# Moving the sums of repeated experts' gates from the routing to the table writes, holding gathers back until the routing is over, and pacing the zeroing

## The chip, the cores and the metric

One NeuronCore of a Trainium2 chip runs the whole program. The metric is device microseconds of one launch; before the change the median of three runs is 4929.35 us (4927.22 to 4931.84). TensorE (PE) does the matrix products, VectorE (DVE) and ScalarE (ACT) the elementwise work, GpSimd (POOL) some elementwise work and all indirect DMAs, and SyncE (SP) issues the plain DMAs.

## The reference: what is computed

Two layers of a diffusion backbone over 512 latent tokens and 256 context tokens (six tiles of 128 tokens), width 1024. Each layer has a modulated norm, one wide input projection, three kinds of attention heads, an output projection with a gated residual, and then PEER, a retrieval of single-neuron experts: 16,384 experts, 8 heads, the best 16 experts of each head for each token.

```
q = (x @ Wq) per head, in two halves; scores of 128 + 128 keys; top 16 of each; top 16 of the sums
e[t, h, k]   expert number,   g[t, h, k] = softmax of the chosen scores
y[t] = sum over h, k of  g[t,h,k] * gelu(x[t] . U[e[t,h,k]]) * V[e[t,h,k]]
```

The kernel computes the sum over experts as dense products wherever that is cheaper: a "P" array or a "table" holds, per token, a number for each of the 16,384 experts, zero nearly everywhere. If two heads of a token choose the same expert, its entry has to hold the sum of both gates. Those sums are what this change moves.

## The kernel before, in words

Layer 0 handles tiles 0 to 5, layer 1 (the last) tiles 0 to 3, since context tokens are not read again. After the attention part of a layer come four stages:

- **Up pass, half 0 and half 1** (`upass`): 64 steps `jj` each. A step loads 512 KB of U, splits it in a high and a low fp16 half (`hl`, on ACT and DVE, or POOL in the first steps) and multiplies with the tokens of the tiles that are done densely (`pw` in half 0, `pa` in half 1, 24 matmuls a step).
- **Value pass, group by group** (`vpass`): 128 steps a group; a step loads 512 KB of V, splits it into `hl` too, and multiplies with the weights of three tiles (layer 0: tiles 2, 3, 4, then 5, 0, 1) or two (layer 1) into `acc`.

The routing (scores, top 16, gates: `routing`, `pick`) runs beside half 0 as a list of generators, `rg`; a step of `upass` advances it by `RRATE`. Three ways lead from the routing to the value pass:

- Tiles 2 and 3 use one-hot products on PE (`Onehot`).
- Tiles 4 and 5 of layer 0 and tile 1 of layer 1 ("dense, with a table") write the gates into a table in DRAM, 8 MB a tile. `Table.clear` zeroes it with 8 DMAs of 1 MB. `Table.put` writes one head: 16 indirect DMAs on POOL, called *puts* below, L1266, `table<-gs,to`, whose offsets are `to` and whose values are `gs`.
- Tiles 0 and 1 of layer 0 and tile 0 of layer 1 ("picked") skip the dense up pass. For each of their 128 experts a token, `gather` reads 128 rows of U by one indirect DMA of 512 KB on POOL (L946, `r<-peer_u,ix`), and DVE makes a dot product with the token (L952, 1024 columns). There are 3 buffers `r`. After 16 dots, gelu and the gate follow, and 16 puts of `a` into the tile's table. All dots of a tile go into one `a`, so the second tile's dots wait for the first tile's last puts.

In all there are 384 gathers and 768 puts. Gathers stand in the list `bg` and puts in the list `sq` (first come first served); a step of `upass` or `vpass` advances them by `RATES[layer]` and `SRATES[layer]`, whose four numbers in use are those of half 0, half 1 and the two groups of the value pass. Every gather and put is tied behind the latest split `hl` by an ordering edge without a semaphore (`queue_behind`), so that the compiler's scheduler, which sorts each engine's instructions by priority, does not pull it to the front. Each engine then runs its queue in that order.

The gate sums are made in `pick` (L921, tile `gjk`): for each of the 128 chosen experts of a token one DVE instruction compares it with all 128 (`is_equal`), multiplies with the gates and adds up. It does so for each of the six tiles that have a table (four in layer 0, two in layer 1), right after the routing of that tile, 768 in all.

Of the kernel before, what the change touches and what calls it, by code (L numbers as in the profile page):

```python
# [31 lines left out]
RATE_NA, RATE_DF = 2.7, 1.4  # L32
RATES = {0: (0.8, 1.0, 1.5, 1.5, 0.0, 0.0), 1: (0.6, 1.2, 0.4, 0.8, 0.0, 0.0)}
SRATES = {0: (2.0, 2.9, 1.6, 1.8, 4.0, 4.0), 1: (1.5, 1.8, 0.9, 1.2, 4.0, 4.0)}
RRATE = (1.3, 1.05)
# [6 lines left out]
ZC = 2048  # L42
# [5 lines left out]
class Hybrid:  # L48
# [22 lines left out]
    def consts(self):  # L71
# [13 lines left out]
        self.tok = c.tile([128, 1], F32, name="tok")  # L85
        nc.gpsimd.iota(self.tok, pattern=[[0, 1]], base=0, channel_multiplier=1, allow_small_or_imprecise_dtypes=True)
        self.mhalf = c.tile([128, 8], F32, name="mhalf")
        nc.vector.memset(self.mhalf, -0.5)
# [181 lines left out]
    def mixers(self, l, last, wes):  # L270
# [11 lines left out]
        with ExitStack() as e:  # L282
            nap = self.pool(e, "nqkv")
            self.naT = nap.tile([128, 4, 2, T], F16, name="naT")
            self.nav = [nap.tile([128, 2, 2, 256], F16, name=f"nav{p}") for p in range(3)]
            self.zero = nap.tile([128, ZC // 4], F32, name="zero")
            self.nc.gpsimd.memset(self.zero, 0.0)
            hp = self.pool(e, "hT", 3)
# [75 lines left out]
    def project(self, l, last, hp, pool, ps, ap_, att_es, xs):  # L364
# [3 lines left out]
        def load(ch):  # L368
            res = []
            for k in range(0, KC, 2):  # L370
                w = pool.tile([128, 2, 256], F32, name="wst", bufs=3)
                nc.sync.dma_start(w, wv[:, k:k + 2, ch * 256:ch * 256 + 256])
                h = pool.tile([128, 2, 256], F16, name="wh", bufs=6)
                lo = pool.tile([128, 2, 256], F16, name="wl", bufs=6)
                self.wsplit(h, lo, w)
                res += [(h[:, x], lo[:, x]) for x in range(2)]
            return res
# [441 lines left out]
    def picks(self, l, tiles, sv, si, pool):  # L819
        for t in tiles:  # L820
            yield from self.pick(l, t, sv[t], si[t], pool)
            if t in self.picked:
                self.bg.append(self.gather(l, t))
            elif t in self.tables:
                self.sq += [self.tables[t].put(h, self.rt[t][2], self.rt[t][0], h, 8) for h in range(8)]

# [21 lines left out]
    def pick(self, l, t, sv, si, pool):  # L848
# [25 lines left out]
        st = pool.tile([128, 2, 16, 8], F16, name="st")  # L874
        sg = pool.tile([128, 16, 8], F32, name="sgate")
        sh = [128, 16, 16, 8]
# [27 lines left out]
        if t not in self.tables:  # L904
            self.onehot.prep(t, st.rearrange("p a k h -> p a (k h)"), sg.rearrange("p k h -> p (k h)"))
            self.rt[t] = None
            return
        ef = pool.tile([128, 16, 8], F32, name="ef")
        nc.vector.scalar_tensor_tensor(ef, st[:, 0], 128.0, st[:, 1], op0=OP.mult, op1=OP.add)
        ix = None  # L910
        if t in self.picked:
            ix = self.lp.tile([128, 16, 8], I32, name="ix", bufs=len(self.picked))
            nc.vector.tensor_scalar(ix, ef, float(l * 16384), None, op0=OP.add)
        to = self.lp.tile([128, 16, 8], I32, name="to", bufs=len(self.tables))
        nc.vector.tensor_scalar(to, ef, 128.0, self.tok, op0=OP.mult, op1=OP.add)

        gs = self.lp.tile([128, 16, 8], F32, name="gs", bufs=len(self.tables))
        e, g, o = (z.rearrange("p k h -> p (k h)") for z in (ef, sg, gs))
        for k in range(128):
            jk = pool.tile([128, 128], BF16, name="gjk")  # L920
            nc.vector.scalar_tensor_tensor(jk, e, e[:, k:k + 1], g, op0=OP.is_equal, op1=OP.mult,  # L921
                                           accum_out=o[:, k:k + 1])
            if k % 16 == 15:
                yield
        self.rt[t] = o, ix, to

# [9 lines left out]
    def gather(self, l, t):  # L936
        nc = self.nc
        gs, ix, to = self.rt[t]
        h = self.lp.tile([128, D], F32, name="hg", bufs=1)
# [3 lines left out]
        for k in range(128 + AHEAD):  # L943
# [6 lines left out]
            if k >= AHEAD:  # L950
                r, d = rows[k - AHEAD], k - AHEAD
                nc.vector.scalar_tensor_tensor(r, r, 1.0, h, op0=OP.mult, op1=OP.mult,  # L952
                                               accum_out=a[:, d // 16, d % 16:d % 16 + 1])
                if d % 16 == 15:
                    x = a[:, d // 16]
                    nc.scalar.activation(x, x, AF.Gelu)
                    nc.vector.tensor_tensor(x, x, gs[:, d // 16::8], op=OP.mult)
                    self.sq.append(self.tables[t].put(d // 16, to, x, 0, 1))
            yield
# [64 lines left out]
    def upass(self, l, half, ps, tag, rrate, more=None):  # L1024
# [18 lines left out]
        for jj in range(64):  # L1043
# [24 lines left out]
            self.tick(self.rg, rrate)  # L1068
            self.tick(self.bg, RATES[l][half])
            self.tick(self.sq, SRATES[l][half])  # L1070
# [163 lines left out]
class Table:  # L1234
# [19 lines left out]
    def clear(self):  # L1254
        o = self.o
        for c in range(0, 128 * 128, ZC):
            self.before.append(o.nc.sync.dma_start(self.view()[:, c:c + ZC].rearrange("i (r n) -> i r n", r=4),
                                                  o.zero[:, None].to_broadcast([128, 4, ZC // 4])))
            yield

    def put(self, h, to, values, c, step):
        o = self.o
        key = f"{self.key}_{h}"
        now = []
        for k in range(16):
            ins = o.nc.gpsimd.indirect_dma_start(  # L1266
                out=self.d, out_offset=bass.IndirectOffsetOnAxis(ap=to[:, k, h:h + 1], axis=0),
                in_=values[:, c + step * k:c + step * k + 1], in_offset=None)
            if k:
# [85 lines left out]
```

## Time and profile before

| | |
|---|---|
| median of 3 runs | 4929.35 us (4927.22 to 4931.84) |
| profiled run | 4932.08 us, span of the trace 4930.0 us, mean granted TensorE clock 0.921 |
| layer 0: attention part | 0 to 611 us |
| layer 0: up pass, half 0 / half 1 | 611 to 1186 / 1186 to 1618 us |
| layer 0: value pass, group 1 / group 2 | 1618 to 2437 / 2437 to 2944 us |
| layer 1: attention part | 2944 to 3405 us |
| layer 1: up pass, half 0 / half 1 | 3405 to 3875 / 3875 to 4191 us |
| layer 1: value pass | 4191 to 4930 us |

The stages' times come from the starts of their first splits `hl`. Times are microseconds from the start of the span. "Busy" is time in which an engine works; "idle before" is time in which it stood still just before an instruction, with what ended that time behind the arrow ("issue": nothing that the profile shows). A granted clock of 1.00 is TensorE at 2.4 GHz; a smaller number is a stretch in which part of the time was granted at 1.2 GHz.

### The profile page before, as it was taken

What the parts mean: (1) busy time and instruction counts of PE and PEld (TensorE: products, weight loads), DVE (VectorE), ACT (ScalarE), POOL (GpSimd) and SP (SyncE); (2) the same over time, 40 slices, a digit from 0 to 9 for tenths busy, and PEclk for the clock granted to TensorE, in tenths of its full rate; (3) what the DMA queues carried; (4) which work ended last, traced back from release to release, by engine and by line L of the source; (5) the groups of instructions that cost most, each with busy time, mean ns of one, the idle gap of its engine ahead of it and who ended that gap; (6) DMA issues with size and microseconds to landing.
All of it is one profiled execution on the core that took longest, in us unless ns stands there. A gap on an engine that the chain in (4) does not pass through costs nothing. (4 is left out here: it accounts for less than half of the span.)

```text
span 4930.0 us, 74817 instructions
## 1 busy us (share of the span) xinstructions
PE 4154.8 (84%) x27326; PEld 2287.3 (46%) x27326; DVE 3391.1 (69%) x7913; ACT 1981.4 (40%) x3236; POOL 1877.5 (38%) x1536
## 2 busy tenths in 40 slices
PE   4987888987898889567599999978879888999998
PEld 3664453753444334222244447745546445444443
DVE  7677559889555776566466554574698867987665
ACT  4556353432222334112233336564525322554444
POOL 4224214303777774567500002251213577761000
PEclk8997898998999989878799999978989999999999
DMA  7831343324667887977778863114446678777887
GB/s 250 298 127 35 131 124 100 111 75 129 196 207 214 256 263 224 337 262 262 228 252 269 259 219 102 50 42 135 125 127 190 214 255 267 264 259 253 265 270 238
DMA packets 512322, 971.54 MB, mean 197 GB/s; under 512 B 73824, under 2 KB 295488, under 8 KB 511952
## 3 DMA queue, kind: packets, MB, share of 16 engines
q1 hardware_dynamic: 422464, 759.66, 48.0%
q0 software_dynamic: 80032, 201.86, 12.8%
q10 hardware_dynamic: 9456, 5.24, 0.4%
q8 instruction: 214, 3.51, 0.3%
q14 instruction: 156, 1.28, 0.1%
HBM read 861.77 MB, written 104.78 MB: 196 GB/s over the span
## 5 line engine op out<-in xcount | busy, mean ns | idle before, releaser
L1141 PE MATMUL acc<-hl,gst 128*128 128x512 f16 x7680 | 1761.7, 391 | 231.2 <-ACT gst L140 151.7
L1141 PEld LDWEIGHTS <-gst 128*128 128x128 f16 x7680 | 760.8, 100 | 1201.4 <-issue 179.6
L1054 PEld LDWEIGHTS <-hl 128*128 128x128 f16 x6144 | 613.3, 101 | 726.4 <-DVE hl L144 128.7
L1127 ACT ACTIVATE hl<-s 128x1024 f16<-128x1024 f32 x512 | 538.4, 1053 | 748.0 <-PE acc L1141 393.9
L952 DVE SCALAR_TENSOR_TENSOR r<-r,hg 128x1024 f32<-128x1024 f32 x384 | 468.7, 1224 | 458.1 <-DMA r<-peer_u,ix 457.1
L946 POOL DMA_INDIRECT r<-peer_u,ix x384 | 481.8, 1255 | 665.6 <-DVE r L952 240.0
L1128 DVE TENSOR_TENSOR hl<-s,hl 128x1024 f16<-128x1024 f32 x512 | 625.4, 1222 | 140.8 <-ACT hl L1127 138.7
L1054 PE MATMUL pw<-h2Uh,hl 128*128 128x512 f16 (+1 forms) x2048 | 601.9, 371 | 83.4 <-DVE hl L144 71.0
L1054 PE MATMUL pa<-h2Uh,hl 128*128 128x512 f16 (+1 forms) x2048 | 584.2, 363 | 49.7 <-DVE hl L144 49.4
L1266 POOL DMA_INDIRECT table<-a,to x384 | 494.0, 1286 | 172.4 <-issue 122.3
L1266 POOL DMA_INDIRECT table<-gs,to x384 | 470.1, 1224 | 201.9 <-issue 128.8
L161 POOL TENSOR_TENSOR rstd<-rstd,mhalf 128x1 f32<-128x1 f32 x26 | 14.6, 562 | 1117.2 <-DVE rstd L160 1114.5
L1054 PE MATMUL pw<-h2Ul,hl 128*128 128x512 f16 (+1 forms) x1024 | 379.2, 370 | 0.0
L1054 PE MATMUL pa<-h2Ul,hl 128*128 128x512 f16 (+1 forms) x1024 | 371.7, 363 | 0.0
L169 PE MATMUL pj<-wh,hTl 128*128 128x256 f16 x1072 | 295.8, 276 | 3.0 <-DVE hTl L142 2.5
L167 PE MATMUL pj<-wh,hTh 128*128 128x256 f16 x1072 | 295.8, 276 | 1.2 <-ACT hTh L140 1.2
L168 PE MATMUL pj<-wl,hTh 128*128 128x256 f16 x1072 | 296.0, 276 | 0.0
L144 DVE SCALAR_TENSOR_TENSOR hl<-s,hl 128x1024 f16<-128x1024 f32 x208 | 255.8, 1231 | 19.2 <-ACT hl L140 19.1
L1061 ACT ACTIVATE gst<-pa 128x512 f32<-128x512 f32 (+1 forms) x128 | 69.5, 543 | 486.2 <-PE pa L1054 383.7
L154 POOL TENSOR_TENSOR wl<-wst,wh 128x512 f16<-128x512 f32 x96 | 125.3, 1319 | 287.7 <-ACT wh L153 248.8
L140 ACT ACTIVATE hl<-s 128x1024 f16<-128x1024 f32 x208 | 219.1, 1053 | 11.8 <-DMA s<-ut 10.7
L154 POOL TENSOR_TENSOR hl<-s,hl 128x1024 f16<-128x1024 f32 x48 | 106.3, 2218 | 290.0 <-ACT hl L153 264.5
(292 smaller groups left out, 7000.5 us busy)
## 6 DMA issues: line engine op xcount, KB each, us to landing
s<-peer_v SPq DMA_DIRECT2D x512, 512.0 KB, 4.6
s<-ut SPq DMA_DIRECT2D x256, 512.0 KB, 4.3
table<-zero SPq DMA_DIRECT2D x48, 1024.0 KB, 7.7
wq<-peer_wq SPq DMA_DIRECT2D x128, 256.0 KB, 3.7
spill<-gst SPq DMA_DIRECT2D x112, 256.0 KB, 4.5
wst<-w_in SPq DMA_DIRECT2D x96, 256.0 KB, 3.1
h2Ul<-table SPq DMA_DIRECT2D x192, 128.0 KB, 3.5
h2Uh<-table SPq DMA_DIRECT2D x192, 128.0 KB, 3.4
```

Source lines behind the costliest of these rows:

```text
L144: return nc.vector.scalar_tensor_tensor(lo, src, scale, hi, op0=OP.mult, op1=OP.subtract)
L154: return (lo_eng or nc.gpsimd).tensor_tensor(lo, w, hi, op=OP.subtract)
L167: nc.tensor.matmul(out, ah, bh, start=start, stop=False)
L168: nc.tensor.matmul(out, ah, bl, start=False, stop=False)
L169: nc.tensor.matmul(out, al, bh, start=False, stop=stop)
L946: self.queue_behind(nc.gpsimd.indirect_dma_start(out=r, out_offset=None, in_=self.i["peer_u"], in_offset=bass.IndirectOffsetOnAxis(ap=ix[: ...
L952: nc.vector.scalar_tensor_tensor(r, r, 1.0, h, op0=OP.mult, op1=OP.mult, accum_out=a[:, d // 16, d % 16:d % 16 + 1])
L1054: nc.tensor.matmul(pa[:, c:d], uh[:, x, k], h[:, k, c:d], start=k == 0 and i == 0, stop=k == KC - 1 and i == 2)
L1127: nc.scalar.activation(vh[:, 0], v, AF.Copy)
L1128: self.lo_ins = nc.vector.tensor_tensor(vh[:, 1], v, vh[:, 0], op=OP.subtract)
L1141: nc.tensor.matmul(acc[s][hf], pr[:, w, s, j % 2], vh[:, x, hf * 512:hf * 512 + 512], start=j == 0 and i == 0, stop=j == 127 and i == 2)
L1266: ins = o.nc.gpsimd.indirect_dma_start(out=self.d, out_offset=bass.IndirectOffsetOnAxis(ap=to[:, k, h:h + 1], axis=0), in_=values[:, c + s ...
```

## The change: what it does

1. The sums leave `pick`. `entries(t, h)` makes the 16 sums of one head and the head's offsets `to` (128 x 16) when they are due: for tiles 4, 5 and layer 1's tile 1 when the put of that head starts, for picked tiles at the ninth dot of the head. `gs` and `to` are now small tiles with four buffers each, shared by all tables; the sums' unused output `oj` has one buffer, under a name that it shares with a tile of the one-hot path.
2. In the up pass the gathers get rate 0 while the routing list is not empty. `RATES` and `SRATES` get new numbers.
3. The tile of zeros is kept for the whole run and is 128 x 128 instead of 128 x 512, so the same 1 MB goes out in pieces of 512 B instead of 2 KB; the zeroing DMAs are now tied behind the latest split too (and the splits of the projection's weights count as such).

```
-RATES = {0: (0.8, 1.0, 1.5, 1.5, 0.0, 0.0), 1: (0.6, 1.2, 0.4, 0.8, 0.0, 0.0)}
-SRATES = {0: (2.0, 2.9, 1.6, 1.8, 4.0, 4.0), 1: (1.5, 1.8, 0.9, 1.2, 4.0, 4.0)}
+RATES = {0: (1.0, 1.4, 1.4, 1.4, 0.0, 0.0), 1: (1.0, 1.2, 0.5, 0.9, 0.0, 0.0)}
+SRATES = {0: (3.0, 2.6, 1.6, 1.8, 4.0, 4.0), 1: (2.5, 1.8, 0.9, 1.2, 4.0, 4.0)}
...
+        self.zero = c.tile([128, ZC // 16], F32, name="zero")
+        nc.gpsimd.memset(self.zero, 0.0)
...
-            self.zero = nap.tile([128, ZC // 4], F32, name="zero")
-            self.nc.gpsimd.memset(self.zero, 0.0)
...
-                self.wsplit(h, lo, w)
+                self.lo_ins = self.wsplit(h, lo, w)
...
-                self.sq += [self.tables[t].put(h, self.rt[t][2], self.rt[t][0], h, 8) for h in range(8)]
+                self.sq += [self.put(t, h) for h in range(8)]
+
+    def entries(self, t, h):
+
+        nc = self.nc
+        _, e, g = self.rt[t]
+        o = self.lp.tile([128, 16], F32, name="gs", bufs=4)
+        to = self.lp.tile([128, 16], I32, name="to", bufs=4)
+        for k in range(16):
+            jk = self.sp.tile([128, 128], F16, name="oj", bufs=1)
+            nc.vector.scalar_tensor_tensor(jk, e, e[:, k * 8 + h:k * 8 + h + 1], g, op0=OP.is_equal, op1=OP.mult,
+                                           accum_out=o[:, k:k + 1])
+        nc.vector.tensor_scalar(to, e[:, h::8], 128.0, self.tok, op0=OP.mult, op1=OP.add)
+        return o, to
+
+    def put(self, t, h):
+        o, to = self.entries(t, h)
+        yield from self.tables[t].put(h, to, o)
...
-        to = self.lp.tile([128, 16, 8], I32, name="to", bufs=len(self.tables))
-        nc.vector.tensor_scalar(to, ef, 128.0, self.tok, op0=OP.mult, op1=OP.add)
-
-        gs = self.lp.tile([128, 16, 8], F32, name="gs", bufs=len(self.tables))
-        e, g, o = (z.rearrange("p k h -> p (k h)") for z in (ef, sg, gs))
-        for k in range(128):
-            jk = pool.tile([128, 128], BF16, name="gjk")
-            nc.vector.scalar_tensor_tensor(jk, e, e[:, k:k + 1], g, op0=OP.is_equal, op1=OP.mult,
-                                           accum_out=o[:, k:k + 1])
-            if k % 16 == 15:
-                yield
-        self.rt[t] = o, ix, to
+        self.rt[t] = ix, ef.rearrange("p k h -> p (k h)"), sg.rearrange("p k h -> p (k h)")
...
+                if d % 16 == 8:
+                    gs, to = self.entries(t, d // 16)
...
-                    nc.vector.tensor_tensor(x, x, gs[:, d // 16::8], op=OP.mult)
-                    self.sq.append(self.tables[t].put(d // 16, to, x, 0, 1))
+                    nc.vector.tensor_tensor(x, x, gs, op=OP.mult)
+                    self.sq.append(self.tables[t].put(d // 16, to, x))
...
-            self.tick(self.bg, RATES[l][half])
+            self.tick(self.bg, 0 if self.rg else RATES[l][half])
...
-            self.before.append(o.nc.sync.dma_start(self.view()[:, c:c + ZC].rearrange("i (r n) -> i r n", r=4),
-                                                  o.zero[:, None].to_broadcast([128, 4, ZC // 4])))
+            ins = o.nc.sync.dma_start(self.view()[:, c:c + ZC].rearrange("i (r n) -> i r n", r=16),
+                                      o.zero[:, None].to_broadcast([128, 16, ZC // 16]))
+            o.queue_behind(ins)
+            self.before.append(ins)
```

How the queues change, at three places. The first is DVE's queue in layer 0's half 0 of before, where the sums of the second dense tile stand (`gjk,gs<-ef,sgate`, each such instruction one sum; `hl` is a step's split).

```order
L909 SCALAR_TENSOR_TENSOR ef<-st 128x128
L915 TENSOR_SCALAR to<-ef,tok 128x128
L921 SCALAR_TENSOR_TENSOR gjk,gs<-ef,sgate 128x128 x80
L144 SCALAR_TENSOR_TENSOR hl<-s_9910,hl 128x1024
L921 SCALAR_TENSOR_TENSOR gjk,gs<-ef,sgate 128x128 x16
L144 SCALAR_TENSOR_TENSOR hl<-s_9977,hl 128x1024
L921 SCALAR_TENSOR_TENSOR gjk,gs<-ef,sgate 128x128 x32
L144 SCALAR_TENSOR_TENSOR hl<-s_10076,hl 128x1024
```

In the changed kernel DVE's queue has the sums (`oj,gs<-ef,sgate`) singly or a few together among the top-16 operations of the routing in half 0 (L846 to L850).

```order
L848 MATCH_REPLACE rest<-sv,sc 128x128
L846 MAX sv<-sc 128x8
L849 MAX sv<-rest 128x8
L847 MAX_INDEX si<-sv,sc 128x8
L850 MAX_INDEX si<-sv,rest 128x8
L848 MATCH_REPLACE rest<-sv,sc 128x128
L835 SCALAR_TENSOR_TENSOR oj,gs<-ef,sgate 128x128
L849 MAX sv<-rest 128x8
L835 SCALAR_TENSOR_TENSOR oj,gs<-ef,sgate 128x128
L850 MAX_INDEX si<-sv,rest 128x8
L156 TENSOR_TENSOR wql<-wq,wqh 128x512
```

Of the 256 sums of the two dense tiles that stood ahead of the first picked tile's indices `ix` (L913), 97 still do, and 18 splits `hl` instead of 32; the rest come later, head by head.

The second place is POOL's queue in layer 0 around the first gather, of before.

```order
L154 TENSOR_TENSOR hl<-s_9374,hl 128x1024
L1266 DMA table_4_102<-gs,to 2097152x1 x68
L946 DMA r<-peer_u,ix 128x1024
L1266 DMA table_4_102<-gs,to 2097152x1 x2
L946 DMA r<-peer_u,ix 128x1024
L1266 DMA table_4_102<-gs,to 2097152x1 x2
```

And of the changed kernel, the same place and then a place some 100 rows on, within half 1, where gathers run alone and the first picked tile's puts and the second dense tile's come.

```order
L1277 DMA table_4_104<-gs,to 2097152x1 x3
L156 TENSOR_TENSOR hl<-s_9901,hl 128x1024
L1277 DMA table_4_104<-gs,to 2097152x1 x57
L953 DMA r<-peer_u,ix 128x1024
L1277 DMA table_4_104<-gs,to 2097152x1 x3
...
L1277 DMA table_5_105<-gs,to 2097152x1 x2
L953 DMA r<-peer_u,ix 128x1024 x27
L1277 DMA table_0_102<-a,to 2097152x1 x2
...
L1277 DMA table_0_102<-a,to 2097152x1 x3
L1277 DMA table_5_105<-gs,to 2097152x1 x16
L953 DMA r<-peer_u,ix 128x1024 x2
L1277 DMA table_5_105<-gs,to 2097152x1 x16
```

Ahead of the first gather stand 72 puts instead of 68. Behind it before has about three puts to each gather until the dense tiles are written; the changed kernel has stretches of gathers alone (27 in one row) and then heads of 16 puts at once.

The third place is DVE's queue of the changed kernel late in half 1 of layer 0, with what each instruction waits for; `DMASW` are the queues of POOL's indirect DMAs, and L959 is a picked tile's dot.

```order
L146 SCALAR_TENSOR_TENSOR hl<-s_17165,hl 128x1024 [waits DMAHW2_49,PE_49,Activation_49]
L959 SCALAR_TENSOR_TENSOR r,a<-r,hg 128x1024 [waits DMASW1_49]
L837 TENSOR_SCALAR to<-ef,tok 128x16 [waits DMASW6_49,DMASW3_49,DMASW7_49,DMASW2_49,DMASW0_49]
L1240 TENSOR_TENSOR P<-pw,P 128x64x8 [waits PE_49]
L146 SCALAR_TENSOR_TENSOR hl<-s_17228,hl 128x1024 [waits DMAHW4_49,Activation_49]
L1221 TENSOR_TENSOR oi<-iox,sT 128x1024
```

In before DVE waits for puts only where the next picked tile's dots take over `a`. Now the offsets `to` of a head wait until the puts of the head four places earlier have landed, since they take over its buffer (33 of the 48 such writes wait so), and the splits `hl` behind them in DVE's queue wait too.

The zeroing DMAs of layer 0 move back within layer 0's projection on SP's queue; those of layer 1 move from layer 0's value pass into layer 1's projection.

## Rows read from the trace of the kernel before

**Rows 1.** The page's busy time, share of the span and instructions of each engine.

```profile
PE 4154.8 (84%) x27326; PEld 2287.3 (46%) x27326; DVE 3391.1 (69%) x7913; ACT 1981.4 (40%) x3236; POOL 1877.5 (38%) x1536
```

**Rows 2.** Windows: start:end, length, then each engine's busy us.

```profile
core 0: us, PE busy (x) PEld busy (x) DVE busy (x) ACT busy (x) POOL busy (x), PEclk, DMA share, GB/s
850.00:900.00 50.00, 45.51 (x346) 25.99 (x345) 49.69 (x287) 12.27 (x23) 35.26 (x32) 0.93 0.26 78
950.00:1000.00 50.00, 50.00 (x675) 40.78 (x674) 40.79 (x190) 22.75 (x47) 0.00 (x0) 1.00 0.41 124
1050.00:1100.00 50.00, 32.82 (x125) 13.26 (x124) 48.22 (x256) 16.79 (x26) 0.00 (x0) 0.84 0.26 79
1300.00:1400.00 100.00, 92.08 (x519) 42.68 (x518) 56.85 (x84) 24.78 (x33) 77.94 (x64) 0.97 0.72 212
1927.00:2067.00 140.00, 98.61 (x427) 41.39 (x426) 82.32 (x118) 32.15 (x38) 65.88 (x56) 0.86 0.96 336
1950.00:2270.00 320.00, 210.74 (x765) 82.28 (x763) 197.06 (x295) 62.24 (x69) 194.09 (x154) 0.82 0.86 295
2600.00:2944.00 344.00, 343.64 (x1591) 155.32 (x1589) 200.13 (x248) 127.29 (x131) 0.00 (x0) 1.00 0.78 249
2944.00:3245.00 301.00, 262.30 (x2553) 206.11 (x2553) 148.49 (x273) 182.70 (x330) 67.86 (x60) 0.97 0.26 79
```

**Rows 3.** TensorE's waits (us in all, times, longest): 1186-1240, 2384-2470, 3590-3700 us.

```profile
PE pa L1054 <- DVE hl L144: 23.4, 1, 23.4
...
PE acc L1141 <- ACT gst L140: 37.2, 2, 36.6
...
PE pw L1054 <- DVE hl L144: 33.5, 3, 22.7
```

**Rows 4.** Timeline of POOL: around the first gather, and layer 0's last gather.

```profile
917.50 0.96 POOL L1266 DMA_INDIRECT table<-gs,to  x1 [0.31 <-issue]
...
1119.69 1.05 POOL L946 DMA_INDIRECT r<-peer_u,ix  x1 [201.23 <-DVE ix L913]
...
2384.02 1.22 POOL L946 DMA_INDIRECT r<-peer_u,ix  x1 [0.30 <-issue]
```

**Rows 5.** Groups on POOL (busy us, mean ns | idle before us), 798 to 914 us.

```profile
L1266 POOL DMA_INDIRECT table<-gs,to x65 | 71.6, 1101 | 43.6 <-issue 25.6 <-DVE gjk L921 17.1 <-DVE st L884 0.3
```

**Rows 6.** Groups of POOL's instructions, 1240 to 1600 us (half 1).

```profile
L1266 POOL DMA_INDIRECT table<-gs,to x164 | 199.2, 1215 | 76.8 <-issue 53.6 <-DMA table<-gs,to 21.4 <-DMA r<-peer_u,ix 1.8
L946 POOL DMA_INDIRECT r<-peer_u,ix x57 | 65.5, 1150 | 17.4 <-issue 14.9 <-DVE hl L144 1.2 <-DVE oj L1212 0.6
```

**Rows 7.** Groups of POOL's instructions, 1973 to 2384 us (second picked tile).

```profile
L946 POOL DMA_INDIRECT r<-peer_u,ix x123 | 154.8, 1258 | 101.7 <-DVE r L952 68.4 <-issue 17.7 <-DVE hl L1128 7.7
L1266 POOL DMA_INDIRECT table<-a,to x96 | 121.8, 1269 | 33.2 <-issue 27.8 <-DMA table<-a,to 5.5
```

**Rows 8.** DVE's longest wait, whole run: total us, times, longest.

```profile
DVE r L952 <- DMA r<-peer_u,ix: 457.1, 168, 8.7
```

**Rows 9.** Timeline of DVE in the first block of sums: start, duration.

```profile
859.80 0.35 DVE L921 SCALAR_TENSOR_TENSOR gjk<-ef,sgate 128x128 bf16<-128x128 f32 x1
...
860.07 0.35 DVE L921 SCALAR_TENSOR_TENSOR gjk<-ef,sgate 128x128 bf16<-128x128 f32 x1
```

**Rows 10.** Timeline of DVE, two accumulating products with one output buffer.

```profile
103.43 1.23 DVE L193 SCALAR_TENSOR_TENSOR wjk<-h2T,h2T 128x1024 f16<-128x1024 f32 x1 [7.52 <-DMA h2T<-w_ada]
...
104.70 1.22 DVE L193 SCALAR_TENSOR_TENSOR wjk<-h2T,h2T 128x1024 f16<-128x1024 f32 x1
```

**Rows 11.** Groups of DVE's splits in 2384 to 2470 and in 2600 to 2944 us.

```profile
L1128 DVE TENSOR_TENSOR hl<-s,hl 128x1024 f16<-128x1024 f32 x10 | 12.2, 1223 | 6.9 <-ACT hl L1127 6.7
...
L1128 DVE TENSOR_TENSOR hl<-s,hl 128x1024 f16<-128x1024 f32 x87 | 106.3, 1223 | 59.2 <-ACT hl L1127 57.3 <-DMA h2Ul<-table 1.9
```

**Rows 12.** The zeroing DMAs: durations, first and last start, and time to landing.

```profile
L1257 SPq DMA_DIRECT2D table<-zero x48: 417/460/1689, 61.7 to 2067.3; - x48
...
DMA to landing us min/median/max: 5.9/7.7/11.7
```

More of the change, by code (lines that the diff above doesn't have):

```diff
@@ L874, in pick @@
         st = pool.tile([128, 2, 16, 8], F16, name="st")
-        sg = pool.tile([128, 16, 8], F32, name="sgate")
+        own, n = (self.lp, len(self.tables)) if t in self.tables else (pool, 2)
+        sg = own.tile([128, 16, 8], F32, name="sgate", bufs=n)
         sh = [128, 16, 16, 8]
@@ L907, in pick @@
             return
-        ef = pool.tile([128, 16, 8], F32, name="ef")
+        ef = self.lp.tile([128, 16, 8], F32, name="ef", bufs=n)
         nc.vector.scalar_tensor_tensor(ef, st[:, 0], 128.0, st[:, 1], op0=OP.mult, op1=OP.add)
@@ L937, in gather @@
         nc = self.nc
-        gs, ix, to = self.rt[t]
+        ix, _, _ = self.rt[t]
         h = self.lp.tile([128, D], F32, name="hg", bufs=1)
@@ L1256, in clear, with put @@
         for c in range(0, 128 * 128, ZC):
-            self.before.append(o.nc.sync.dma_start(self.view()[:, c:c + ZC].rearrange("i (r n) -> i r n", r=4),
-                                                  o.zero[:, None].to_broadcast([128, 4, ZC // 4])))
+            ins = o.nc.sync.dma_start(self.view()[:, c:c + ZC].rearrange("i (r n) -> i r n", r=16),
+                                      o.zero[:, None].to_broadcast([128, 16, ZC // 16]))
+            o.queue_behind(ins)
+            self.before.append(ins)
             yield
-    def put(self, h, to, values, c, step):
+    def put(self, h, to, values):
         o = self.o
@@ L1266, in put @@
             ins = o.nc.gpsimd.indirect_dma_start(
-                out=self.d, out_offset=bass.IndirectOffsetOnAxis(ap=to[:, k, h:h + 1], axis=0),
-                in_=values[:, c + step * k:c + step * k + 1], in_offset=None)
+                out=self.d, out_offset=bass.IndirectOffsetOnAxis(ap=to[:, k:k + 1], axis=0),
+                in_=values[:, k:k + 1], in_offset=None)
             if k:
```

## The prediction, made before the changed kernel ran

> **What bounds the kernel now.** I read the page's busy times first, then windows, then the waits and groups of the engine that each window points to. TensorE is busy for 4154.8 of 4930 us [rows 1], so about 775 us at most can be won by filling its holes, and a little more by its clock. The windows show where it is full: 50.0 of 50 us in 950 to 1000 and 343.64 of 344 us at the end of layer 0, both at a granted clock of 1.00 [rows 2]. There nothing that this change touches can gain anything. It is not full in three kinds of stretch:
>
> - Half 0 of each layer, while a tile's sums stand on DVE: in 850 to 900 us DVE is busy 49.69 of 50 and in 1050 to 1100 us 48.22, TensorE only 32.82 in the latter at a clock of 0.84 [rows 2]. The waits name DVE's `hl`: 23.4 us at 1186 to 1240 us, and 33.5 us in layer 1 at 3590 to 3700 us [rows 3].
> - Half 1: TensorE is 92.08 of 100 us busy in 1300 to 1400 us [rows 2].
> - The value pass while the second picked tile is gathered: 210.74 of 320 us, clock 0.82 [rows 2].
>
> In the last two the limit is POOL's queue, although the page shows POOL busy for only 38% [rows 1]. In 1240 to 1600 us, 164 puts cost 199.2 us busy and 76.8 us idle, 57 gathers 65.5 and 17.4 [rows 6]: 359 of 360 us. So a put really takes 276.0 / 164 = 1.68 us of queue and a gather 82.9 / 57 = 1.45. In 1973 to 2384 us the queue is full as well: 154.8 + 101.7 + 121.8 + 33.2 = 411.5 us for 123 gathers and 96 puts [rows 7], 3.34 us for each gather, 68.4 us of it waiting for DVE's dots. DVE in turn waits for gathered rows, 457.1 us in the whole run [rows 8]: its queue is in order, so the splits `hl` that TensorE needs stand behind a dot whose rows are not there.
>
> That queue starts late. The first gather ends an idle time of 201.23 us on POOL at 1119.69 us, waiting for DVE's `ix`, and the puts of the first dense tile, the last of which started at 917.50 us, stood behind it [rows 4]. From there to the last gather of layer 0 at 2384.02 us [rows 4] are 1264 us. By the order there are 412 puts and 256 gathers in it: 412 x 1.68 + 256 x 1.45 = 692 + 371 = 1063 us of work, so 201 us of idle time.
>
> **The change part by part.** The sum is made against the profiled run, 4932.1 us, which is 2.7 us above the median.
>
> *Fewer sums before the first gather.* A sum takes 0.27 us from start to start (859.80 to 860.07) [rows 9]. Ahead of `ix` 159 sums fewer stand on DVE, 159 x 0.27 = 43 us, and 14 splits fewer, at 1.22 us each [rows 11] 17 us. The one buffer of the sums' output makes a sum that follows another wait for its end: two products with one buffer start 1.27 us apart at a length of 1.23 us [rows 10], so 0.04 us past the end, while the sums now start 0.08 us before it (0.35 long). That is 0.12 us for each of those sums that stand in a row, some 3 us of the 97 left. Together -57 us: the first gather comes at about 1063. The bounds are 0 (TensorE is full in 950 to 1000 us [rows 2], so DVE's time may be worth nothing there) and -60. I take -57, because 14 steps of TensorE go out of the way too.
>
> *POOL's queue from first to last gather.* The changed order has 409 puts and 256 gathers there: 409 x 1.68 + 256 x 1.45 = 1058 us. The idle time is worked out by stretches. (a) 27 gathers run without a put at 1.4 a step, about 19 steps; a step of half 1 took 432 us / 64 = 6.75 us, and TensorE filled 92.08 of 100 of it [rows 2], which leaves 6.2; 19 x 6.2 = 118, less 27 x 1.45 = 39: 79 us. (b) In the pause between the two picked tiles 34 steps of the value pass at 344 / 87 = 3.95 us [rows 2, 11] give 134 us, with 53 puts and 5 gathers in them, 96 us: 38 us. (c) In the burst after it, 76 gathers stand within 24 steps with 36 puts. The work is 76 x 1.45 + 36 x 1.68 = 171 us; at before's 3.34 us a gather it would take 254, which is 83 idle, and with the waits for dots alone (68.4 / 123 x 76) 42 idle. I take 70, nearer to the former. (d) By the order five heads' puts come next on POOL when their offsets still wait for the puts four heads earlier to land. DVE's waits for an indirect DMA were 457.1 / 168 = 2.7 us in the mean and 8.7 at most [rows 8], so 14 to 44 us; I take 17. The sum is 79 + 38 + 70 + 17 = 204 us, and the last gather comes at 1063 + 1058 + 204 = 2325, that is 59 us earlier. The bounds are -110 (no idle time but that of before's burst) and +30 (two round trips for each of 16 heads).
>
> *What is left behind the last gather.* In before 10 splits follow in 2384 to 2470 us [rows 11] and TensorE waits 37.2 us there [rows 3]. The change of group so cost 86 - 10 x 3.95 = 46 us, of which that wait is most. In the changed order the last dot stands 21 splits earlier, so about 30 steps x 3.95 = 118 us follow; with 14 us left for the change of group, since nothing from POOL is late then, 132 us against 86: +46. Bounds +42 (without the wait) and +79 (all of it stays).
>
> *Sums beside the dots.* 512 sums of layer 0 now stand in DVE's queue in half 0 and 1. Where DVE waits for rows anyhow (457.1 us [rows 8]), they cost nothing; where that cover ends, 415 sums that were ahead of or beside the routing cost the same 0.27 to 0.39 us later. I take 0; bounds -10 and +40.
>
> *Zeroing.* 48 DMAs of 1 MB, 7.7 us to landing, from 61.7 to 2067.3 us [rows 12]. The sixteen of layer 1 ran in 1927 to 2067 us, where the DMA share was 0.96 and TensorE busy 98.61 of 140 us; they go to a stretch with a share of 0.26 [rows 2]. Taken at -6: TensorE lost 41 us in those 140, but 1950 to 2270 us, two thirds of it without zeros, lost 109 of 320 [rows 2], about the same share, so nearly all of it is POOL's doing. Bounds -30 and +10. Pieces of 512 B instead of 2 KB are not in the trace; bounds 0 and +10 for layer 0's projection, I take 0, since the zeros only have to be there before the first put at about 798 us [rows 5].
>
> *Layer 1.* 160 sums leave the way of the routing there, 44 us of DVE, beside a hole of 33.5 us [rows 3], of which I take half, -17. They return in half 1, +9. So -8, bounds -44 and +30.
>
> The sum: -59 + 46 + 0 - 6 + 0 - 8 = -27, so 4932.1 - 27 = 4905 us, and 4902 against the median.
>
> [...]
>
> **Rivals.**
>
> *A, slower, 4965 us.* The four buffers of `gs` and `to` tie DVE to POOL. 33 writes of `to` wait for puts; if 13 more of them than I counted are late by 5 us, POOL stands for 65 us more and nothing of the earlier start is left: 4902 + 65 = 4967. A second price of it is the clump of 84 puts in about 12 steps at the end of half 1: 84 x 1.68 + 19 x 1.45 = 169 us against 12 x 6.2 = 74 us of TensorE. For it speaks that DVE's `hl` stand behind these waits; against it that most of these writes stand right behind a dot whose rows were issued after the puts in question. It decides from 25 us of POOL's idle time before `table`, released by DVE's `to` or `oj`, on.
>
> *B, a larger gain, 4830 us.* Puts get cheaper without clumps of sums and with fewer gathers between: 1.50 us as in 798 to 914 us, (71.6 + 25.6) / 65 [rows 5]. 409 x 0.18 = 74 us: 4902 - 74 = 4828. For it: the cheaper put was measured. Against: it was measured with DMA at a share of 0.26, not 0.72 [rows 2].
>
> *C, no change, 4929 us.* The work of POOL's queue is the same, 1058 against 1063 us, and TensorE's full stretch before 1050 us absorbs the earlier sums; what starts earlier then only waits longer.
>
> *D, slower by the port, 4975 us.* If a put had to wait for the sum that runs, half of 0.35 us for each of 409 puts would be 72 us. Against it: in 798 to 914 us DVE was busy with sums nearly without a gap (49.69 of 50 [rows 2]) and a put took 1101 ns [rows 5], against 1215 ns in half 1 [rows 6], where DVE is busy 56.85 of 100 us [rows 2]. The puts beside sums were the faster ones.
>
> **How the numbers follow.** Forecast 0.42 (own range 4875 to 4925), A 0.27, B 0.13, C 0.12, D 0.03, anything else 0.03. Within 0.2% means within 10 us, about what a measurement of this kernel can tell from no change. Faster: 0.37 of the forecast, all of B, 0.01 of the rest, 0.51. Same: 0.05 of the forecast, 0.02 of A, 0.10 of C, 0.17. Slower: 0.25 of A, 0.02 of C, D and 0.02, 0.32. The range reaches over A and B and leaves out their far ends: 4832 to 4985.
>
> **What would show it.** First gather at 1055 to 1075 us, with POOL's idle time before it under 150 us; last gather of layer 0 at 2300 to 2350 us; the wait for `gst` at the change of groups gone; a put at 1.6 to 1.7 us of queue in half 1. The forecast is wrong if the first gather is not earlier than 1100 us, if POOL waits more than 45 us for `to` and `oj`, if puts take 1.5 us (B), or if layer 1 moves by more than 40 us.

## The result, and the profile after

The changed kernel takes 4879.30 us (median of 4 runs, 4865.18 to 4880.65) against 4928.28 us: 0.9899 of before, 95% interval 0.9873 to 0.9925. That is 49 us faster; 27 were forecast. The profiled run is the fastest of the four, 4865.2 us, so the two profiles lie 67 us apart, 18 more than the medians; stage times below are those of the profiles, one trace for each kernel.

The same windows as in [rows 2], of the changed kernel (start:end, length, busy us of PE, PEld, DVE, ACT, POOL, then granted clock, DMA share, GB/s):

```profile
1050.00:1100.00 50.00, 45.64 (x198) 19.85 (x197) 41.90 (x149) 15.69 (x27) 38.42 (x33) 0.93 0.63 191
1300.00:1400.00 100.00, 87.14 (x504) 41.00 (x503) 79.30 (x199) 23.34 (x32) 56.99 (x47) 0.95 0.79 247
1950.00:2270.00 320.00, 229.11 (x952) 93.33 (x951) 240.90 (x493) 74.68 (x92) 234.44 (x186) 0.85 0.82 272
2600.00:2944.00 344.00, 327.57 (x1672) 162.32 (x1670) 193.69 (x270) 138.74 (x177) 11.35 (x13) 0.98 0.70 224
```

In 1050 to 1100 us POOL is already at work (38 us busy, it was 0) and TensorE is 46 us busy instead of 33. The last window now holds the change of layer, because everything is earlier by then.

POOL's first gather and layer 0's last one, in the timeline of the changed kernel:

```profile
1051.46 0.99 POOL L953 DMA_INDIRECT r<-peer_u,ix  x1 [120.59 <-DVE ix L931]
...
2266.92 1.11 POOL L953 DMA_INDIRECT r<-peer_u,ix  x1 [0.30 <-DVE oj L835]
```

Against [rows 4] the first gather comes 68 us earlier and the last one 117 us earlier, so the queue between them takes 1215 us instead of 1264.

What TensorE waited for between the last gather and the second group of the value pass, 2267 to 2412 us (us in all, times, longest):

```profile
PE acc L1150 <- ACT hl L1136: 18.4, 1, 18.4
...
PE acc L1150 <- ACT gst L142: 1.1, 1, 1.1
```

The 37.2 us for `gst` in [rows 3] are gone, and 18.4 us for a split stand there instead. The ninth split of group 2 of layer 0, at which the prediction's 86 us behind the last gather end, starts at 2412 us on DVE (2470 before), layer 1's first split on DVE at 3535 (3599), and the span ends at 4863 (4930). (The group's first split on DVE starts at 2385 us, 2424 before, and not at the 2437 us that the table of stages gives.) So 58 of the 67 us are won in layer 0 up to that ninth split, 6 from there to layer 1's first split on DVE, 3 after it.

POOL's groups in half 1, 1240 to 1600 us (busy us, mean ns | idle before), which answer to [rows 6]:

```profile
L1277 POOL DMA_INDIRECT table<-gs,to x84 | 94.1, 1120 | 42.8 <-issue 22.9 <-DVE oj L835 6.7 <-DVE oj L1221 6.3
L953 POOL DMA_INDIRECT r<-peer_u,ix x70 | 82.3, 1175 | 86.9 <-DVE r L959 47.4 <-DVE oj L835 28.5 <-issue 9.8
L1277 POOL DMA_INDIRECT table<-a,to x34 | 41.8, 1230 | 17.6 <-issue 13.5 <-DMA table<-a,to 3.5 <-DMA r<-peer_u,ix 0.6
```

There are fewer puts in this stretch than before (118, it was 164) and more gathers (70, it was 57), and the gathers now wait for dots. At its end is a new hole. The waits of TensorE and of DVE in 1480 to 1680 us:

```profile
PE pw L1231 <- DVE og L1225: 53.5, 6, 17.0
...
DVE to L837 <- DMA table<-gs,to: 47.4, 3, 18.8
```

Three writes of `to` hold DVE for 47.4 us until puts have landed, and TensorE stands behind DVE for 53.5. That is the clump of 84 puts in which heads of 16 follow each other.

### The profile page after: what moved, and what is told of

Its sections match the earlier page's. It is cut to its first block, busy times and chain, and to the rows that moved or that the text cites. A ratio compares the mean times of both kernels' runs of the same rounds, so it can differ in the third digit from the quotient of the medians.

```text
span 4863.3 us, 75025 instructions
## 1 busy us (share of the span) xinstructions
PE 4123.6 (85%) x27326; PEld 2283.8 (47%) x27326; DVE 3427.9 (70%) x7955; ACT 1982.8 (41%) x3238; POOL 1837.4 (38%) x1535
## 5 line engine op out<-in xcount | busy, mean ns | idle before, releaser
L1150 PE MATMUL acc<-hl,gst 128*128 128x512 f16 x7680 | 1730.9, 387 | 162.2 <-DVE hl L1137 62.1
L959 DVE SCALAR_TENSOR_TENSOR r<-r,hg 128x1024 f32<-128x1024 f32 x384 | 469.2, 1224 | 297.1 <-DMA r<-peer_u,ix 296.4
L953 POOL DMA_INDIRECT r<-peer_u,ix x384 | 476.3, 1240 | 531.4 <-DVE r L959 264.3
L1063 PE MATMUL pw<-h2Uh,hl 128*128 128x512 f16 (+1 forms) x2048 | 592.1, 366 | 37.6 <-DVE hl L146 19.4
L1277 POOL DMA_INDIRECT table<-gs,to x384 | 426.9, 1112 | 214.7 <-issue 90.0
L835 DVE SCALAR_TENSOR_TENSOR oj<-ef,sgate 128x128 f16<-128x128 f32 x768 | 271.8, 354 | 13.9 <-DVE r L959 0.8
```

What stands on the lines that cost most here:

```text
L835: nc.vector.scalar_tensor_tensor(jk, e, e[:, k * 8 + h:k * 8 + h + 1], g, op0=OP.is_equal, op1=OP.mult, accum_out=o[:, k:k + 1])
L953: self.queue_behind(nc.gpsimd.indirect_dma_start(out=r, out_offset=None, in_=self.i["peer_u"], in_offset=bass.IndirectOffsetOnAxis(ap=ix[: ...
L1063: nc.tensor.matmul(pa[:, c:d], uh[:, x, k], h[:, k, c:d], start=k == 0 and i == 0, stop=k == KC - 1 and i == 2)
L1150: nc.tensor.matmul(acc[s][hf], pr[:, w, s, j % 2], vh[:, x, hf * 512:hf * 512 + 512], start=j == 0 and i == 0, stop=j == 127 and i == 2)
L1277: ins = o.nc.gpsimd.indirect_dma_start(out=self.d, out_offset=bass.IndirectOffsetOnAxis(ap=to[:, k:k + 1], axis=0), in_=values[:, k:k + 1] ...
```

## The experiments

The theory at the start was that the sums had held up POOL's queue, and that their move was nearly the whole gain. Rival theories were the zeroing (layer 1's 16 MB beside the gathers) and the new rates with the rule that gathers wait for the routing. Six runs took one part, two parts or a single line of the change.

**The sums alone.** Edit: `entries` and `put` as in the change, rates and zeroing as before.

> The kernel before with the sums moved alone (entries, put, four buffers of gs and to); rates and zeroing as before. Theory 1 (the sums held up the start of POOL's queue): most of the gain is here, 0.990 to 0.995 of before (-25 to -49 us), first gather before 1080 us instead of 1119.7. Theory 2 (the zeroing of layer 1's tables beside the gathers was the cost) and theory 3 (the rates and the rule that gathers wait for the routing are the gain): 0.998 to 1.004, since neither is touched.

Measured: 4898.99 us against 4918.75, 0.9955 (0.9935 to 0.9974), just outside the 0.990 to 0.995 of theory 1: the sums alone are not most of the gain.

**The rates alone.**

```
-RATES = {0: (0.8, 1.0, 1.5, 1.5, ...), 1: (0.6, 1.2, 0.4, 0.8, ...)}
+RATES = {0: (1.0, 1.4, 1.4, 1.4, ...), 1: (1.0, 1.2, 0.5, 0.9, ...)}
-SRATES = {0: (2.0, 2.9, ...), 1: (1.5, 1.8, ...)}
+SRATES = {0: (3.0, 2.6, ...), 1: (2.5, 1.8, ...)}
-            self.tick(self.bg, RATES[l][half])
+            self.tick(self.bg, 0 if self.rg else RATES[l][half])
```

> The kernel before with the new RATES and SRATES and the rule that gathers get rate 0 while the routing lasts; sums and zeroing as before. Theory 1: 0.997 to 1.005, the first gather stays at 1100 to 1125 us behind 256 sums. Theory 3: 0.990 to 0.995. Theory 2: 1.00.

Measured: 4885.83 us, 0.9920 (0.9889 to 0.9951). Theory 1 had this at no change, so as a whole it falls. The gain was predicted right for theory 3.

The first gather in the timelines of POOL, of the sums alone, then of the rates alone, then of the last line of the rates alone (the run after this one):

```profile
1047.76 0.99 POOL L953 DMA_INDIRECT r<-peer_u,ix  x1 [151.08 <-DVE ix L931]
```

```profile
1121.60 1.05 POOL L946 DMA_INDIRECT r<-peer_u,ix  x1 [107.45 <-DVE ix L913]
```

```profile
1119.97 1.05 POOL L946 DMA_INDIRECT r<-peer_u,ix  x1 [169.22 <-DVE ix L913]
```

The sums alone bring the first gather 72 us forward, with only 48 puts ahead of it instead of 68 (the change has 72). The rates leave it where it was, but POOL's idle time before it falls from 201 to 107 us, since 133 puts run ahead of it. POOL's groups in 910 to 1125 us of the rates alone:

```profile
L1266 POOL DMA_INDIRECT table<-gs,to x72 | 74.5, 1034 | 32.6 <-issue 30.8 <-DVE sv L832 0.9 <-DMA table<-gs,to 0.6
L946 POOL DMA_INDIRECT r<-peer_u,ix x2 | 2.1, 1037 | 107.8 <-DVE ix L913 107.5 <-issue 0.3
```

72 puts there, at (74.5 + 32.6) / 72 = 1.49 us; in before six followed 910 us. So the two parts let work of POOL's queue begin earlier in two ways: the sums by an earlier first gather, the rates by puts that no longer stand behind it. Layer 0's last gather, of the sums alone and then of the rates alone:

```profile
2316.01 1.14 POOL L953 DMA_INDIRECT r<-peer_u,ix  x1 [0.30 <-DVE oj L835]
```

```profile
2335.23 0.94 POOL L946 DMA_INDIRECT r<-peer_u,ix  x1 [1.71 <-DVE r L952]
```

From the first gather to the last, POOL's queue takes 1268 us with the sums alone and 1214 with the rates alone, against 1264 before [rows 4]: the sums start it earlier, the rates make it shorter.

**One line of the rates alone.** Edit: only the last pair of lines of the diff above.

> The kernel before with one line of the rates' part: gathers get rate 0 while the routing lasts; all numbers old. With the rates alone 133 puts instead of 68 ran before the first gather, at the same 1121 us. If that is the gain: 0.990 to 0.995 and more than 100 puts ahead of the first gather. If the new numbers are the gain (fewer puts a step in half 1, gathers sooner after the pause): 0.998 to 1.002.

Measured: 4892.48 us, 0.9950 (0.9933 to 0.9967), at the upper end of what was expected if the line is the gain. 92 puts run ahead of the first gather, fewer than I had expected. The interval overlaps that of the whole rates' part, so what the new numbers add is not told from nothing.

**The zeroing alone.** Edit: the last part of the change (pieces of 512 B, tied behind splits).

> The kernel before with the zeroing in 512-byte pieces and tied behind the splits, sums and rates as before. Theory 1: -15 to +5 us, 0.997 to 1.001, the gathers of 1973 to 2384 us take about 3.3 us each as in before. Theory 2: -25 us or more, gathers at 2.8 us each there as in the changed kernel.

Measured: 4928.01 us, 1.0014 (0.9999 to 1.0029): no gain, and theory 2 falls. The gathers of the second tile in this kernel, 1963 to 2366 us, go as in [rows 7], 403 / 125 = 3.2 us each:

```profile
L946 POOL DMA_INDIRECT r<-peer_u,ix x125 | 160.6, 1285 | 124.0 <-DVE r L952 94.8 <-issue 17.1 <-DVE hl L1128 4.7
```

It does shorten POOL's queue, from 1264 to 1235 us: in before a MEMSET of the second tile of zeros waits in that queue at 1926 us,

```profile
POOL zero L287 <- DVE gst L142: 27.9, 1, 27.9
```

and here it is gone. The ninth split of group 2 comes 18 us earlier with it (2452 us), and 15 of these are lost again by the end of the span; these are single traces.

**The change without its zeroing, and without its rates.** Edits: the lines of the one part put back.

> The changed kernel with the zeroing of before (2 KB pieces, not tied, layer 1's in layer 0's value pass). By then: the sums alone gave 0.9955 of before, the rates alone 0.992, the zeroing alone 1.0014. If the zeroing is worth nothing here either: 0.986 to 0.992, as the changed kernel (0.990) or a little below. If it pays once the gathers come closer together (layer 1's 16 MB then stand beside them): 0.993 to 0.997, and gathers of the second tile's burst at over 3 us each against 2.65 to 2.85 in the changed kernel.

> The changed kernel with the old RATES and SRATES and without the rule that gathers wait for the routing. If the two gains add (the rates shift gathers and puts against each other whenever the queue starts): 0.995 to 0.999, that is 25 to 45 us above the changed kernel. If the sums' earlier start does what the rates did (both only start POOL's queue earlier): 0.988 to 0.992.

Measured: sums and rates 4874.34 us against 4923.24, 0.9909 (0.9880 to 0.9939); sums and zeroing 4900.58 us, 0.9961 (0.9946 to 0.9976). The changed kernel had 0.9899. So the zeroing adds nothing that can be told, and the rates are worth some 30 us beside the sums as well: the two gains add, as the first reading of the second expectation had it. In the kernel with the old zeroing, layer 1's zeros run beside the gathers in 2061 to 2218 us. That window of it, and the same stage of the changed kernel without zeros:

```profile
2061.00:2218.00 157.00, 121.81 (x499) 49.58 (x498) 119.72 (x251) 40.84 (x44) 118.19 (x91) 0.92 0.99 369
```

```profile
2051.00:2208.00 157.00, 125.26 (x515) 51.81 (x516) 123.18 (x257) 42.26 (x46) 121.53 (x96) 0.91 0.86 287
```

With the DMA engines busy at a share of 0.99 TensorE does 3.5 us less in 157; that is one pair of windows, and the time of the kernels does not show it. Sums and rates alone would give 0.9955 x 0.9920 = 0.9875 if they simply multiplied; measured is 0.991, and by the intervals of the three ratios this difference is not clear of noise. The traces tell more. Layer 0's last gather of the kernel with sums and rates:

```profile
2276.55 1.11 POOL L953 DMA_INDIRECT r<-peer_u,ix  x1 [0.30 <-DVE oj L835]
```

It comes 107 us earlier than in before, nearly the 68 of the sums alone and the 49 of the rates alone together, so in POOL's queue the parts add up. The ninth split of group 2 comes 46 us earlier, against 44 with the sums alone and 51 with the rates alone, so in TensorE's steps of layer 0 they do not: 32 splits then stand behind the last gather up to that mark, 20 and 12 with one part, 10 in before. Part of an earlier end of POOL's queue so only leaves more steps behind it. These are single traces; by the medians (20, 33 and 49 us) the gains of the whole run nearly add.

**Eight buffers for `gs` and `to`.** Edit to the changed kernel (the tile of zeros also goes back to the projection's pool, which makes the room):

```
-        o = self.lp.tile([128, 16], F32, name="gs", bufs=4)
-        to = self.lp.tile([128, 16], I32, name="to", bufs=4)
+        o = self.lp.tile([128, 16], F32, name="gs", bufs=8)
+        to = self.lp.tile([128, 16], I32, name="to", bufs=8)
```

> The changed kernel with eight buffers of gs and to instead of four (the tile of zeros goes back to the projection's pool to make room, still 128 x 128). In the changed kernel DVE waits 53.5 us in 9 waits of to for puts and TensorE stands 64 us between 1560 and 1680 us. Theory A (the four buffers cost what is left of the possible gain): -20 to -50 us against the changed kernel, 4830 to 4860. Rival (POOL's queue is full there anyhow, the wait is cover): within 10 us of the changed kernel, 4870 to 4890.

Measured: 4843.07 us against 4918.75, 0.9832 (0.9797 to 0.9867), as theory A had it. DVE's wait for `to` in the whole run, and TensorE's wait for `og` in 1480 to 1680 us, are

```profile
DVE to L837 <- DMA table<-gs,to: 6.2, 4, 2.2
...
PE pw L1231 <- DVE og L1225: 2.7, 3, 1.9
```

instead of 53.5 us in 9 waits and 53.5 in 6. The kernel is some 35 us faster than the changed one; by the two ratios it is 33 us, give or take 22. The edit also moves the tile of zeros, and what that alone does to the time is not known (see the slower chip below); the two waits are what the buffers set. The wait was no cover for anything: POOL's last gather of layer 0 moved from 2267 to 2228 us.

**The dots' outputs head by head.** Edit, on top of eight buffers:

```
-        a = self.lp.tile([128, 8, 16], F32, name="a", bufs=1)
...
+                if d % 16 == 0:
+                    a = self.lp.tile([128, 16], F32, name="a", bufs=8)
...
```

> The changed kernel with eight buffers of gs and to, and the dots' outputs in eight tiles of one head each instead of one tile of eight heads (same memory), so that the second picked tile's dots wait for the first tile's puts head by head. With eight buffers alone the second tile's gathers stood from 1684 to 1834 us. If that pause leaves work for a burst that TensorE then waits for: 15 to 40 us below eight buffers alone (4843), 4800 to 4830. If POOL's queue only fills up elsewhere: within 10 us of it, 4833 to 4853.

Measured: 4784.81 us against 4923.24, 0.9720 (0.9686 to 0.9754), the fastest kernel of this study (timed on one chip only), 58 us below eight buffers alone, more than the expected 15 to 40. With eight buffers alone POOL stood at the start of the second tile; its next gather, the fourth of the tile, and the same one of this kernel:

```profile
1833.79 1.71 POOL L953 DMA_INDIRECT r<-peer_u,ix  x1 [52.20 <-DVE r L959]
```

```profile
1699.87 1.71 POOL L952 DMA_INDIRECT r<-peer_u,ix  x1 [5.71 <-DVE r L960]
```

It comes 134 us earlier, and the gathers of the second tile are then spread over the steps of the value pass. The window that [rows 2] had at 210.74 us of TensorE and a clock of 0.82 reads, in this kernel:

```profile
1950.00:2270.00 320.00, 275.50 (x1194) 116.78 (x1194) 225.47 (x417) 106.43 (x122) 219.71 (x167) 0.95 0.80 267
```

**Four runs on a slower chip.** The last four ran together on another chip, on which the kernel before took 4978.01 us.

> The changed kernel with the tile of zeros in the projection's pool, four buffers of gs and to: the control for eight buffers, which had this edit too. If eight buffers were the gain of eight slots (0.9832 of before): 0.987 to 0.993, as the changed kernel. If the place of the tile was: 0.981 to 0.986.

> The changed kernel with the dots' outputs in a tile for each head, and four buffers of gs and to. If the two waits are separate (offsets for puts that have not landed, dots of the second tile for the first tile's puts): 0.976 to 0.981, the 55 us that the edit gave beside eight buffers. If the edit pays only where eight buffers let the heads run ahead: 0.985 to 0.991.

> Eight buffers and a tile for each head, and 4 puts a step instead of 3 in half 0 of layer 0: 96 puts stand ahead of the first gather instead of 72, in which POOL was idle for 123.7 us. If puts made there shorten POOL's queue behind it: 24 x 1.68 = 40 us earlier last gather and 10 to 30 us less, 4755 to 4775. If the sums that they need delay the indices by as much: 4780 to 4800.

> The same with 6 puts a step: 144 puts ahead of the first gather, 72 more than 72. By the first reading the 72 x 1.5 = 108 us fit into POOL's idle time of 123.7 us and the last gather comes 80 to 120 us earlier, 4700 to 4760; by the second, with 64 to 80 sums more ahead of the indices (about 25 us) and the first gather as much later: 4775 to 4800.

Edits: the tile of zeros allocated in the projection's pool; the per-head `a` with four buffers of `gs` and `to`; and, on the fastest kernel, `SRATES` of layer 0's half 0 at 4 and at 6 instead of 3. Measured: 5009.63 us, 1.0063 (1.0029 to 1.0097); 4939.78 us, 0.9927 (0.9903 to 0.9950); 4924.61 us, 0.9891 (0.9866 to 0.9917); 4981.62 us, 1.0000 (0.9980 to 1.0020). None of the expected figures came out. The changed kernel itself was not run on this chip, so the first is no control of times. What its trace does tell: DVE waits for `to` as in the changed kernel, which the place of the tile so leaves alone, and eight buffers are what took that wait away:

```profile
DVE to L837 <- DMA table<-gs,to: 53.5, 9, 18.8
```

Inside the group the kernel with the per-head `a` is 70 us faster than the first. The two also differ in the place of the tile of zeros, so the 70 us are not the per-head `a` alone; but the wait that it takes away is gone with four buffers too. The fourth gather of the second tile, in the first kernel of the group and in the second:

```profile
1955.21 1.71 POOL L953 DMA_INDIRECT r<-peer_u,ix  x1 [72.87 <-DVE r L959]
```

```profile
1804.73 1.72 POOL L952 DMA_INDIRECT r<-peer_u,ix  x1 [3.85 <-DVE r L960]
```

Six puts a step were 57 us worse than four: 144 puts ahead of the first gather, but it came at 1184 us instead of 1131, and the second reading of that expectation is nearer. Four against three was not compared on one chip. All four traces show a wait that the ten others don't have: TensorE idle for 124 to 171 us and DVE for 102 to 126 us with nothing in the profile that ends it ("issue", "remote"), where the other ten have 2.3 us at most. TensorE's rows in the first of them, 889 to 894 us, and POOL's beside them:

```profile
889.54 0.26 PE L167 MATMUL rw<-h2Uh,wqh 128*128 128x128 f16 x1 [1.85 <-issue]
890.27 0.26 PE L168 MATMUL rw<-h2Ul,wqh 128*128 128x128 f16 x1 [0.47 <-issue]
892.38 0.27 PE L169 MATMUL rw<-h2Uh,wql 128*128 128x128 f16 x1 [1.85 <-issue]
893.79 0.26 PE L167 MATMUL rw<-h2Uh,wqh 128*128 128x128 f16 x1 [1.14 <-issue]
```

```profile
888.91 0.96 POOL L1277 DMA_INDIRECT table<-gs,to  x1 [0.30 <-issue]
890.17 1.70 POOL L1277 DMA_INDIRECT table<-gs,to  x1 [0.30 <-issue]
892.18 0.96 POOL L1277 DMA_INDIRECT table<-gs,to  x1 [0.31 <-issue]
897.20 0.96 POOL L1277 DMA_INDIRECT table<-gs,to  x1 [4.06 <-DVE oj L835]
```

Matmuls that follow each other at 0.1 us elsewhere start 0.7 to 2.1 us apart here. Of this idle time of TensorE 122 of 124 us end within 2 us after one of POOL's indirect DMAs, while 38% of the span lies so close behind one. That is a coincidence in time and no cause: from 895.2 us on the matmuls follow each other at 0.1 us again, also beside the puts that go out from 897.2 us on. Why this happens on that chip and not on the others stays open, and none of the times of these four kernels can be set against those of the others.

## Why the prediction was right, point by point

The direction was right and the size a little over half. The mechanism of the sums, an earlier first gather and with it an earlier last one, is seen in the traces, but the sums alone gave only 20 us; that the whole came out 49 us faster rests as much on the rates, which the prediction gave no price of their own. So far the forecast was lucky. By the steps:

- *Fewer sums ahead of the first gather*, -57: measured -68 (1051.5 us). That it needs the sums' move is shown: 1047.8 with the sums alone, 1121.6 with the rates alone.
- *The sums' one output buffer*, 0.12 us: seen. Two in a row, in DVE's timeline of the changed kernel, start 0.38 us apart, 0.27 in [rows 9]:

```profile
885.11 0.34 DVE L835 SCALAR_TENSOR_TENSOR oj<-ef,sgate 128x128 f16<-128x128 f32 x1
...
885.49 0.35 DVE L835 SCALAR_TENSOR_TENSOR oj<-ef,sgate 128x128 f16<-128x128 f32 x1
```

- *POOL's queue from first to last gather*, 1058 us of work and 204 idle: this is the term that was mis-sized. Measured are 1215 us, 47 less; with the sums alone the queue takes 1268, so what the prediction missed is mostly what the rates do. Three of its prices were too high. The 27 gathers without a put took 101 us, 62 above their work and not 79. In the burst I took 70 us idle; it ran 76 gathers and 36 puts in 217 us, 46 above their work. The 3.34 us a gather that I leaned on there hold 96 puts to 123 gathers, and the burst has 36 to 76. Priced apart from [rows 7], a gather at (154.8 + 101.7) / 123 = 2.09 and a put at (121.8 + 33.2) / 96 = 1.61, the burst comes to 76 x 2.09 + 36 x 1.61 = 217 us, as measured. And a put is not always 1.68 us. POOL's groups of the changed kernel in the clump, 1500 to 1650 us:

```profile
L1277 POOL DMA_INDIRECT table<-gs,to x48 | 49.1, 1022 | 14.8 <-issue 14.0 <-DVE og L1225 0.5 <-DVE r L959 0.3
L1277 POOL DMA_INDIRECT table<-a,to x33 | 39.8, 1206 | 17.3 <-issue 13.2 <-DMA table<-a,to 3.5 <-DMA r<-peer_u,ix 0.6
```

  Heads in a row cost (49.1 + 14.8) / 48 = 1.33 us a put, puts between gathers (39.8 + 17.3) / 33 = 1.73. Rival B, the cheaper put, was so true of these heads; all puts of half 1 together still cost 1.66, and B's 4830 us did not come.
- *The wait for buffers*, 17 us: the wait was there, but on another engine. The forecast had it in POOL's queue, where from the first to the last gather of layer 0 only 8.0 us before puts end with the sums and nothing with `to`; DVE waited 53.5 us in the whole run, and TensorE stood behind it at the clump. Rival A had the wait as the reason for a slower kernel. It cost about 35 us, as far as eight buffers show it, not the 65 that would have eaten the gain. One sign of being wrong came true by the letter, more than 45 us of POOL's waits for `to` and `oj`:

```profile
POOL r L953 <- DVE oj L835: 43.6, 34, 6.6
...
POOL table L1277 <- DVE oj L835: 8.0, 2, 6.7
```

  Most of it stands before gathers, which do not read the sums, so this sign did not tell what it was meant to tell. The 8.0 us before puts are below the 25 at which rival A was to decide.
- *What is left behind the last gather*, +46: measured 145 us against 86, +59. The wait for `gst` is gone as forecast, but the change of groups was not free: 32 splits at 3.95 us make 126 us, and the 18.4 us for a split are the rest.
- *Zeroing*, -6, and *512-byte pieces*, 0: by the ratios the part is worth between +7 us (alone) and -5 us (beside sums and rates), not told from nothing.
- *Layer 1*, -8: from the ninth split of layer 0's second group to the end 2451 us against 2460, -9. The agreement is luck in part: 6 of the 9 lie ahead of layer 1's first split on DVE, and only 3 behind it, where the term was worked out.
- *Sums beside the dots*, 0: DVE's wait for gathered rows fell from 457.1 [rows 8] to 296.4 us, which fits that they went where DVE had waited; no run tests it alone.

The first gather (1051 us) and the last one (2267 us) came ahead of the ranges that were to show the forecast, 1055 to 1075 and 2300 to 2350.

What the prediction did not see is what the rates are worth by themselves. I treated them only as part of the order, and took the 201 us before the first gather as a matter of the sums. The rates alone gave 33 us, with puts that pass the waiting gather, which the order of before had shown plainly: 68 puts, a gather, and then puts behind it. Rival C falls with the interval. Rival D, the port: the puts that stand among sums in 1051 to 1360 us take 1162 ns, 1215 in [rows 6] with no sums beside them. The Trainium skill ("SBUF — State Buffer", section "SBUF: two separate sides") has a VectorE operation with two SBUF inputs shut out a GpSimd operation that reads SBUF; the sums have two such inputs, and no slower put shows here beside them. Whether a put counts as such an operation is not shown.

## What to carry to other kernels

An engine that is 38% busy can still be the bound: count the work and the waits of its queue from the first to the last item of a stage, and ask what stands at the head of the queue while it sleeps. Whatever does not need the late input should be queued ahead of the instruction that waits for it. Look at what is left behind the queue's last item too: here its end came 107 us earlier with sums and rates, and the next group of layer 0 only 46. A price for one item that holds other items in it is good only for the same mix. When a large tile is cut into small ones with few buffers, ask who frees a buffer and how late: here four buffers instead of eight cost about 35 us, and one tile for eight heads, where eight tiles of one head take the same memory, about another 58.

## What was not expected of the hardware

A put's cost on POOL is not one number: 1.33 us in runs of whole heads of `gs`, 1.68 to 1.73 between gathers, by the rows above. Gathers between the puts are not the reason by themselves, for 53 puts of `a` in a row, with no gather among them, in 1727 to 1864 us of the changed kernel cost (65.7 + 25.5) / 53 = 1.72 us:

```profile
L1277 POOL DMA_INDIRECT table<-a,to x53 | 65.7, 1239 | 25.5 <-issue 14.6 <-DMA table<-a,to 7.3 <-DVE oi L1221 3.6
```

Of these, 10.9 us are waits for landings and for DVE; without them it is 1.52. What sets the rest was not tested. On one chip TensorE and DVE stood still, TensorE for 0.8 us in the mean and up to 7.9, for 124 to 171 us in a run, nearly always close behind one of POOL's indirect DMAs, and on the chips of the other ten traces they did not. The kernel before was 1.1% slower there too, but no trace of it was taken there.
